# Split output weights kept in DRAM, with the first gathers and two token tiles of the output projection placed beside the end of attention

## The chip, the cores and the metric

The kernel runs on one core of one Trainium2 chip. The metric is device time in microseconds (us), the median of several executions. Five engines work side by side, each through its own queue in order: PE (TensorE) multiplies, ACT (ScalarE), DVE (VectorE) and POOL (GpSimd) do the elementwise work, and SP (SyncE) issues most transfers. POOL issues transfers too, which run through a queue of their own. SBUF is the core's working memory, PSUM holds what PE produces.

## The reference, cut to what matters

One inference step of a decoder with two head groups, a gated short convolution and a sparse attention, for 1024 prompt tokens and 8 sample tokens with 2048 past rows each:

```python
proj = rms_norm(x, norm_g) @ w_in                 # 1024 -> 3864 columns
b_gate, c_gate, conv_in, z_conv, q, kv, gates, z_attn = split(proj)
conv_branch = b_gate * short_conv(c_gate * conv_in) * silu(z_conv)
kv_cmp = compress_blocks(kv rows, cmp_pe, cmp_w)  # 32 rows -> 1, weights cmp_w
o = g0 * attend(q, kv_cmp) + g1 * attend(q, selected) + g2 * attend(q, window)
attn_branch = o * silu(z_attn)
y = x + concat([conv_branch, attn_branch], -1) @ w_out     # 1024 -> 1024
# the sample tokens: the same, with past rows gathered by page_table
# from cache_cmp (compressed with cmp_w) and cache_slc
```

This change touches the way to the last product, `@ w_out`, and to the compression of the gathered past rows with `cmp_w`. Both are computed in two parts each: an operand is split into a high part, rounded to the type float32r, and a low part, the rest. A product is then high*high + high*low + low*high.

## The kernel before

Everything is one program whose order is written by generators; `merge` takes the next piece of the stream that has used the least of its budget, so that the pieces of two streams alternate on each engine's queue. Up to 230 us the input projection for keys, values and queries runs (`phase0`, with `z_part`). From there two streams alternate. The first is attention, `attn_stream`: 32 units, one for each block of 128 queries and pair of heads, four units per block. A unit computes scores (PE, L796), softmax (DVE L784, ACT L786), scaling of the probabilities by gate and sum (POOL, L841 and L845, tiles P0, P1, P2), transposes (PE, L870), a split of the transposed probabilities into `ph` (ACT) and `pl` (DVE), products with the values (PE, L880), and `mixA` (POOL, L895). `copy` (L75) and `sub` (L79) are the helpers that make every high and low part.

The second stream is first the rest of the input projection for the convolution part (`conv_stream`, to about 648 us, with the weight splits `wh` and `wl`). Behind it stands `prefetch`. It loads the eight row blocks of the left half of `w_out` through SP as float32 (`wor`, 256 KB each, L1330), has ACT and DVE split each into `woh` and `wol`, and does the same with the 16 slices of `cmp_w` (`cw_fetch`, four pieces of 4 x 64 KB, tile `cw2`).

When attention has ended, the first stream becomes `out_stream`: for each half n of the output columns and each tile t of 128 tokens it loads x (`xr`), splits the mixed values (`mh` on ACT, `ml` on POOL, from `mixC` for the first four row blocks and from `mixA` for the others), issues 24 matmuls of 512 columns (L1405 to L1407), adds (DVE) and stores (SP). The second stream becomes `cmp_stream`: gathers of past rows through POOL (`raw`, 1 MB each, two buffers), a copy into another order (`reg`, half on ACT, half on POOL), transposes (L999), splits `xh` (ACT) and `xl` (DVE), products with `cw2` (L1023); then `sample_stream` for the 8 sample tokens. In `out_stream` the splits of the right half's weights stand after tiles t = 2 to 5, from loads issued in tiles t = 0 to 3.

`cmp_w` had also been loaded and split once at the beginning (`cw`, in `phase0`), for the prompt's own compression; that copy is given up before attention.

## Time and profile before

| | |
|---|---|
| time, median of 3 runs | 937.73 us (934.72, 937.73, 938.48) |
| the profiled execution | 939.33 us, of which the span of the trace is 937.6 us |
| mean granted PE clock | 0.976 of full speed |
| PE busy | 873.8 us, 93% of the span |
| DVE busy | 619.4 us, 66% |
| ACT busy | 556.0 us, 59% |
| POOL busy | 404.3 us, 43% |
| transfers | 82.24 MB, 47.60 through SP's queue, 33.56 through POOL's |

The profiled execution stands 1.6 us above the median of the three runs, and 1.7 us of it lie outside the span. PE is the busy engine, so what is to be read is where it isn't busy and what it waited for there. In the profile's slices of 23.4 us PE stands at nine tenths or more nearly everywhere from 260 to 650 us; slices 29 and 30 (about 656 to 703 us) show seven and nine tenths.

### The profile page before, as it was taken

The numbers are of one execution on the slowest core, as the hardware profiler recorded it, in microseconds if no ns is written. First come the engines' busy times: TensorE is split into PE (matmuls) and PEld (weight loads), VectorE is DVE, ScalarE is ACT, GpSimd is POOL, SyncE is SP. The second block draws the span as 40 slices with busy tenths as digits, with TensorE's granted clock in tenths as the row PEclk, the third lists the DMA queues.
The fourth block names the chain that finished last, engine by engine and source line by source line (L and its number), as shares of the span: only waits on it lengthen the run. The fifth ranks groups of instructions, "written<-read, shape, count | busy, mean of one in ns | idle before, by whom it ended". The sixth has DMA issues, their size and how long they took to land.

```text
span 937.6 us, 16976 instructions
## 1 busy us (share of the span) xinstructions
PE 873.8 (93%) x5789; PEld 783.2 (84%) x5789; DVE 619.4 (66%) x1714; ACT 556.0 (59%) x1495; POOL 404.3 (43%) x550
## 2 busy tenths in 40 slices
PE   7988999999899999999989999999679999798998
PEld 6888999999689889898979899998568888576765
DVE  5896734788655555856775686577745555877883
ACT  5764543733665655656556666576757666675761
POOL 4132340311454444444434444343455543477761
PEclk8999989999999999999999999999989999899999
DMA  7513331211011000000000100001495661857631
GB/s 246 154 57 95 95 114 35 80 57 31 6 30 34 24 23 24 23 24 23 13 12 23 24 23 1 23 2 44 127 302 182 214 214 47 314 179 226 214 102 47
DMA packets 57955, 82.24 MB, mean 88 GB/s; under 512 B 14470, under 2 KB 43086, under 8 KB 55692
## 3 DMA queue, kind: packets, MB, share of 16 engines
q1 hardware_dynamic: 50956, 47.60, 16.9%
q0 software_dynamic: 6912, 33.56, 10.6%
q8 instruction: 46, 0.75, 0.3%
q14 instruction: 41, 0.34, 0.1%
HBM read 74.24 MB, written 11.10 MB: 91 GB/s over the span
## 4 chain that ended last, share of the span: by engine, by line
PE 49%; ACT 7%; DVE 7%; POOL 3%; issue 3%; DMA 1%; ACTq 0%; DVEq 0%; POOLq 0%
PE o L880 7%; PE pt L870 5%; PE s L796 5%; PE mm L225 5%; PE mm L224 5%; PE mm L223 5%; POOL P L845 2%; ACT P L786 2%; PE mm L1407 1%; PE pt L999 1%; PE mm L1405 1%; PE mm L1406 1%; PE mm L1023 1%; ACT ph L75 1%; PE o L1278 1%
## 5 line engine op out<-in xcount | busy, mean ns | idle before, releaser
L223 PE MATMUL mm<-hH,wh 128*128 128x384 f32 (+1 forms) x480 | 157.9, 329 | 0.0
L225 PE MATMUL mm<-hH,wl 128*128 128x384 f32 (+1 forms) x480 | 155.7, 324 | 0.0
L224 PE MATMUL mm<-hL,wh 128*128 128x384 f32 (+1 forms) x480 | 155.1, 323 | 0.0
L786 ACT ACTIVATE P<-P,stat 128x640 f32<-128x640 f32 (+7 forms) x192 | 112.9, 590 | 37.4 <-DVE stat L784 36.8
L79 POOL TENSOR_TENSOR wl<-wraw,wh 128x256 fp32r<-128x256 f32 (+1 forms) x120 | 87.7, 749 | 106.2 <-ACT wh L75 96.8
L79 DVE TENSOR_TENSOR pl<-pt,ph 128x512 fp32r<-128x512 f32 (+1 forms) x164 | 102.4, 636 | 45.3 <-ACT ph L75 43.9
L75 ACT ACTIVATE ph<-pt 128x512 fp32r<-128x512 f32 (+1 forms) x164 | 88.3, 549 | 66.1 <-PE pt L870 65.5
L845 POOL TENSOR_SCALAR P<-P,stat,gates 128x640 f32<-128x640 f32 (+7 forms) x128 | 101.1, 800 | 55.8 <-DVE stat L836 52.7
L870 PE MATMUL pt<-ident,P 128*128 128x128 f32 x592 | 95.5, 278 | 6.4 <-POOL P L845 3.5
L796 PE MATMUL s<-k,q 128*128 128x320 f32 (+8 forms) x416 | 95.8, 334 | 3.7 <-DVE q L79 1.5
L208 PE MATMUL mm<-wh,hH 128*128 128x256 f32 (+1 forms) x320 | 93.5, 292 | 0.4 <-ACT hH L75 0.4
L209 PE MATMUL mm<-wl,hH 128*128 128x256 f32 (+1 forms) x320 | 93.2, 292 | 0.2
L210 PE MATMUL mm<-wh,hL 128*128 128x256 f32 (+1 forms) x320 | 93.0, 291 | 0.0
L223 PEld LDWEIGHTS mm<-hH,wh 128*128 128x128 f32 x480 | 91.9, 191 | 0.8 <-DVE mixC L693 0.6
L224 PEld LDWEIGHTS mm<-hL,wh 128*128 128x128 f32 x480 | 91.9, 191 | 0.1
L225 PEld LDWEIGHTS mm<-hH,wl 128*128 128x128 f32 x480 | 91.9, 192 | 0.1
L784 DVE CUSTOM_DVE_ANT_0 P<-s,mask 128x32 f32<-128x32 f32 (+8 forms) x160 | 70.9, 473 | 27.0 <-PE s L796 22.4
L870 PEld LDWEIGHTS pt<-ident,P 128*128 128x128 f32 x592 | 70.0, 140 | 19.9 <-POOL P L845 10.1
L880 PE MATMUL o<-ph,v 128*128 128x256 f32 x264 | 74.5, 301 | 3.6 <-ACT ph L75 3.0
L880 PE MATMUL o<-pl,v 128*128 128x256 f32 x264 | 73.3, 300 | 3.3 <-DVE pl L79 3.2
L796 PEld LDWEIGHTS s<-k,q 128*128 128x128 f32 x416 | 66.8, 190 | 8.1 <-DVE q L79 1.7
L841 POOL TENSOR_SCALAR P<-P,stat,gates 128x32 f32<-128x32 f32 x64 | 22.9, 370 | 94.4 <-DVE stat L836 76.4
(342 smaller groups left out, 2182.9 us busy)
## 6 DMA issues: line engine op xcount, KB each, us to landing
wraw<-in_w_in_dram SPq DMA_DIRECT2D x56, 256.0 KB
xt<-in_x_prompt_dram SPq DMA_DIRECT2D x8, 512.0 KB
wor<-in_w_out_dram SPq DMA_DIRECT2D x16, 256.0 KB
xr<-in_x_prompt_dram SPq DMA_DIRECT2D x16, 256.0 KB
out_y_prompt_dram<-xr SPq DMA_DIRECT2D x16, 256.0 KB
sd<-in_state_win_kv_dram SPq DMA_DIRECT2D x8, 512.0 KB
out_s_win_dram<-in_state_win_kv_dram SPq DMA_DIRECT2D x8, 511.0 KB
cwr<-in_cmp_w_dram SPq DMA_DIRECT2D x32, 64.0 KB
```

What stands on the lines that cost most here:

```text
L75: return ACT.activation(out, in_, AF.Copy)
L79: return eng.tensor_tensor(out, a, b, OP.subtract)
L208: PE.matmul(o[:, :n], hH[t // 3][:, k, s], wh, start=k == 0, stop=False)
L209: PE.matmul(o[:, :n], hH[t // 3][:, k, s], wl, start=False, stop=False)
L223: PE.matmul(o[:, :n], wh, hH[c][:, k], start=k == 0, stop=False)
L224: PE.matmul(o[:, :n], wh, hL[c][:, k], start=False, stop=False)
L225: PE.matmul(o[:, :n], wl, hH[c][:, k], start=False, stop=k == 7)
L786: return lambda: ACT.activation(P, P, AF.Exp, bias=stt[:, 0, c:c + 1], scale=-1.0, accum_out=stt[:, 1, c:c + 1])
L796: PE.matmul(s[:, a:b], q[:, i], k, start=first, stop=not first)
L845: POOL.tensor_scalar(P[:, i, :n], P[:, i, :n], stt[:, 2, c + i:c + i + 1], gates[:, qi, gt:gt + 1], op0=OP.mult, op1=OP.mult)
L870: PE.transpose(p[:, y * 256 + i * 128:y * 256 + i * 128 + 128], src[:, i], ident)
L880: PE.matmul(o[0][:, :256], v, X[:, y * 256:y * 256 + 256], start=br == 1 and x == 0 and y == 0 and X is h[0], stop=last and y + 1 == len(p ...
```

## The change

The split forms are made once, written to DRAM (`wo_d`, eight blocks of 512 KB, and `cw_d`, four of 512 KB), and later loaded whole.

- `phase0`: after each of the four splits of `cw` one SP store of the split slices to `cw_d`.
- `attn_stream`: in units 0 to 15 (blocks 0 to 3, whose probabilities need only half of P1) the free half of P1 serves as scratch. An even unit loads a row block of `w_out`; the next odd unit splits it, high part on ACT, low part on POOL, and SP stores it to `wo_d`. P1 becomes two tiles, P1a and P1b.
- `prefetch`: no loads, splits and waits on ACT and DVE any more; POOL issues eight transfers `wo_d` to SBUF and four `cw_d` to SBUF, and the first two gathers between the latter.
- `early_out`: tiles t = 0 and 1 of the left half are put into the second stream, beside attention's last units. Their buffers are the six tiles q0 to q5 that held the queries: tile 0 takes q0 to q4, tile 1 takes q5 and again q0 to q3.
- `first` waits for `early` before it goes on, `out_stream` skips what was begun, and the right half's weight loads move from tiles 0 to 3 to tiles 2 to 5, each behind its tile's store.

```diff
+    wo_d = [dram.tile([128, 2, 512], F32, name=f"wo_d{k}") for k in range(8)]
+    cw_d = [dram.tile([128, 4, 2, 128], F32, name=f"cw_d{i}") for i in range(4)]
...
             if 0 < t < 5:
                 cw_split()
+            if 1 < t < 6:
+                SP.dma_start(cw_d[t - 2], f(cw[:, t * 4 - 8:t * 4 - 4]))
...
+        def w_split(ui):
+            nonlocal wsp
+            if ui % 2 == 0:
+                wsp = at.tile([128, 2, 512], F32R, name="P1b")
+                SP.dma_start(f(wsp[:, 1]), w_out[:, ui // 2, 0:512])
+            else:
+                copy(ACT, wsp[:, 0], f(wsp[:, 1]))
+                sub(POOL, wsp[:, 1], f(wsp[:, 1]), f(wsp[:, 0]))
+                SP.dma_start(wo_d[ui // 2], f(wsp))
...
-            P1 = at.tile([128, 2, 1024], F32, name="P1")
+            a = at.tile([128, 1024], F32, name="P1a")
+            P1 = (a[:, 0:512], a[:, 512:1024]) if u[0] < 4 else (a, at.tile([128, 1024], F32, name="P1b"))
...
+            if u[0] < 4:
+                w_split(ui)
...
     def prefetch():
...
-        cwp = cmp_rooms()
-        jobs = []
         for k in range(8):
-            jobs.append(lambda k=k: w_piece(0, k, cwp, 4))
-            if k % 2:
-                jobs.append(lambda i=k // 2: cw_fetch(cwp, cw2, i))
-        late = []
-        for j in jobs:
-            late.append(j())
-            if len(late) > 4:
-                late.pop(0)()
-            yield 1000
-        for split in late:
-            split()
-            yield 800
+            w = wop.tile([128, 2, 512], F32R, name=f"wo{k}")
+            POOL.dma_start(w, wo_d[k])
+            wo[0, k] = w[:, 0], w[:, 1]
+            yield PREF
+        for i in range(4):
+            if i < 2:
+                gather(i)
+            POOL.dma_start(cw2[:, i * 4:i * 4 + 4], cw_d[i])
+            yield PREF
...
+    def early_out():
+        homes = [f"q{t}" for t in range(6)]
+        def room(name, dt):
+            homes.append(homes.pop(0))
+            return qkv.tile([128, 512], dt, name=homes[-1])
+        for t in range(EARLY):
+            yield from out_tile(0, t, room)
...
-                if n == 0 and t < 6:
-                    if t < 4:
-                        late.append(w_piece(1, t + 4, op, 2))
-                    if t > 1:
-                        late.pop(0)()
+                def made(n=n, t=t):
+                    if n == 0 and late:
+                        late.pop(0)()
+                    if n == 0 and t - EARLY < 4:
+                        late.append(w_piece(1, t - EARLY + 4, op, 2))
...
+    EARLY, PREF = 2, 400
...
         yield from prefetch()
-        done["weights"] = True
+        yield from early_out()
+        done["early"] = True
```

`out_tile` is the body of the loop in `out_stream`, moved out unchanged but for where its buffers come from. The numbers behind names below are those of buffers; a line number of the changed kernel is some 8 to 25 larger than the same statement's before.

**POOL, around the last two units.** Before, from the second half of the scaling of unit 30's P1 to the `mixA` behind that of unit 31's P1:

```order
L845 TENSOR_SCALAR P_8549<-P_8549,stat,gates 128x1024 [waits Activation_49]
L895 TENSOR_TENSOR mixA<-ot,mixA 128x128 [waits DVE_49]
L841 TENSOR_SCALAR P_3452<-P_3452,stat,gates 128x32 [waits DVE_49,PE_49]
L841 TENSOR_SCALAR P_3452<-P_3452,stat,gates 128x32 [waits PE_49,Activation_49]
L845 TENSOR_SCALAR P_8550<-P_8550,stat,gates 128x640 [waits PE_49,Pool_49]
L845 TENSOR_SCALAR P_8550<-P_8550,stat,gates 128x640
L845 TENSOR_SCALAR P_8749<-P_8749,stat,gates 128x1024 [waits DVE_49,PE_49]
L845 TENSOR_SCALAR P_8749<-P_8749,stat,gates 128x1024 [waits Activation_49]
L895 TENSOR_TENSOR mixA<-ot,mixA 128x128 [waits DVE_49]
```

Now, from behind that scaling to the seventh transfer of `wo_d`:

```order
L1369 DMA wo_8849<-wo_d_79 128x1024
L1369 DMA wo_8870<-wo_d_80 128x1024
L903 TENSOR_TENSOR mixA<-ot,mixA 128x128 [waits DVE_49]
L1369 DMA wo_8872<-wo_d_81 128x1024
L1369 DMA wo_8874<-wo_d_82 128x1024
L849 TENSOR_SCALAR P_3470<-P_3470,stat,gates 128x32 [waits DVE_49,PE_49]
L849 TENSOR_SCALAR P_3470<-P_3470,stat,gates 128x32 [waits PE_49,Activation_49]
L853 TENSOR_SCALAR P_8623<-P_8623,stat,gates 128x640 [waits PE_49,Pool_49]
L853 TENSOR_SCALAR P_8623<-P_8623,stat,gates 128x640
L1369 DMA wo_8885<-wo_d_83 128x1024
L1369 DMA wo_8887<-wo_d_84 128x1024
L1369 DMA wo_8902<-wo_d_85 128x1024
```

Two, two and four issues of transfers now stand between the scalings: the eighth is the next row, then comes the scaling of unit 31's P1, then the first gather, `mixA` and the scaling of unit 31's P0 and P2, and then four transfers of `cw_d` with the second gather between.

**PE, at the scores of the last unit.** Before (P are the probabilities of unit 30, `s` the scores of unit 31):

```order
L731 MATMUL mm<-ident,uo 10x128 [waits DVE_49]
L880 MATMUL o<-ph,v_81 128x256 [waits DVE_49,Activation_49]
L796 MATMUL s<-k_80,q_8667 128x512 [waits DVE_49,PE_49]
L870 MATMUL pt<-ident,P_8549 128x128 [waits DVE_49]
L870 MATMUL pt<-ident,P_8549 128x128 x3
L796 MATMUL s<-k_80,q_8668 128x512
```

Now, in the same place:

```order
L739 MATMUL mm<-ident,uo 10x128 [waits DVE_49]
L888 MATMUL o<-ph,v_95 128x256 [waits DVE_49,Activation_49]
L804 MATMUL s<-k_94,q_8740 128x512 [waits DVE_49,PE_49]
L1397 MATMUL mm<-wo_8849,q_8989 128x512 [waits DMASW0_49,Activation_49]
L878 MATMUL pt<-ident,P1a 128x128 [waits DVE_49]
```

The first matmul of token tile 0 stands between a score and the transposes and waits for the first transfer of POOL (DMASW0); the other 23 are spread over the rest of the two units.

**ACT, where attention ends** (`ot` is the last output of attention). Before, with the splits of the weights between:

```order
L75 ACTIVATE woh_9029<-wor 128x512 [waits DMAHW1_49]
L75 ACTIVATE ph<-pt 128x512 [waits DVE_49,PE_49] x2
L75 ACTIVATE cw_8774<-cwr 128x8x64 [waits DMAHW4_49,DMAHW5_49,DMAHW3_49,DMAHW2_49]
L75 ACTIVATE woh_9035<-wor 128x512 [waits DMAHW6_49]
L75 ACTIVATE woh_9039<-wor 128x512 [waits DMAHW7_49]
L75 ACTIVATE ph<-pt 128x512 [waits DVE_49,PE_49]
L75 ACTIVATE ot<-o 64x128 [waits PE_49]
L75 ACTIVATE ot<-o 64x128
L75 ACTIVATE mh<-mixC 128x512
L75 ACTIVATE mh<-mixA 128x512
```

Now:

```order
L75 ACTIVATE q_9096<-mixA 128x512 [waits PE_49]
L75 ACTIVATE ph<-pt 128x512 [waits PE_49,Activation_49] x3
L75 ACTIVATE ph<-pt 128x512 [waits DVE_49,PE_49] x4
L75 ACTIVATE ot<-o 64x128 [waits PE_49]
L75 ACTIVATE ot<-o 64x128
L75 ACTIVATE q_9092<-mixC 128x512 [waits DMAHW6_49,DVE_49]
L75 ACTIVATE reg<-raw 128x8x64 [waits DMASW0_49,Pool_49]
L75 ACTIVATE reg<-raw 128x8x64
```

The weight splits are gone; the high part of token tile 1 (q_9092, in the buffer q0) stands behind attention's last copy and waits for DMAHW6, the store of tile 0's output from that same buffer, and the copies of the gathered rows are queued behind it.

## Rows read from the trace of the kernel before

**Rows 1.** Busy time by stretch: PE, PEld, DVE, ACT, POOL, clock, DMA share, GB/s.

```profile
240.00:440.00 200.00, 193.89 (x1270) 177.13 (x1270) 117.57 (x411) 123.93 (x391) 95.98 (x176) 0.99 0.09 23
...
660.00:680.00 20.00, 13.46 (x74) 10.28 (x75) 14.20 (x30) 12.81 (x31) 11.03 (x12) 0.95 0.42 123
680.00:700.00 20.00, 15.10 (x77) 12.40 (x76) 10.03 (x13) 11.75 (x22) 13.63 (x14) 0.93 0.95 312
...
720.00:900.00 180.00, 168.92 (x1037) 134.69 (x1035) 123.00 (x244) 121.84 (x254) 105.82 (x103) 0.97 0.59 200
900.00:938.00 38.00, 30.86 (x154) 22.16 (x152) 21.52 (x45) 11.59 (x28) 11.00 (x9) 0.99 0.13 43
```

**Rows 2.** Timeline of PE at attention's end: start, duration, operation [idle before <-releaser].

```profile
659.21 0.38 PE L880 MATMUL o<-ph,v 128*128 128x256 f32 x1 [0.18 <-ACT ph L75]
...
664.54 0.38 PE L880 MATMUL o<-ph,v 128*128 128x256 f32 x1 [1.30 <-ACT ph L75]
...
673.71 0.39 PE L880 MATMUL o<-pl,v 128*128 128x256 f32 x1 [0.81 <-DVE pl L79]
```

**Rows 3.** Timeline of PE behind attention.

```profile
678.12 0.63 PE L1405 MATMUL mm<-woh,mh 128*128 128x512 f32 x1
678.55 0.63 PE L1406 MATMUL mm<-wol,mh 128*128 128x512 f32 x1
...
685.66 0.66 PE L999 MATMUL pt<-ident,reg 128*128 128x128 f32 x4 [1.25 <-ACT reg L75]
...
696.23 0.38 PE L1023 MATMUL mm<-xh,cw 128*128 128x256 f32 x1 [2.99 <-ACT xh L75]
...
702.05 0.39 PE L1405 MATMUL om<-woh,mh 128*128 128x512 f32 x1
702.29 0.40 PE L1406 MATMUL om<-wol,mh 128*128 128x512 f32 x1
```

**Rows 4.** Timeline of ACT from attention's end on.

```profile
656.92 0.62 ACT L75 ACTIVATE woh<-wor 128x512 fp32r<-128x512 f32 x1
...
689.99 0.63 ACT L75 ACTIVATE cw<-cwr 128x512 fp32r<-128x512 f32 x1 [0.67 <-DMA cwr<-in_cmp_w_dram]
...
694.54 0.63 ACT L75 ACTIVATE woh<-wor 128x512 fp32r<-128x512 f32 x1 [2.36 <-DMA wor<-in_w_out_dram]
```

**Rows 5.** Timeline of POOL from unit 30 to the first gathers.

```profile
644.23 2.38 POOL L845 TENSOR_SCALAR P<-P,stat,gates 128x1024 f32<-128x1024 f32 x2 [6.68 <-DVE stat L836]
...
659.92 2.39 POOL L845 TENSOR_SCALAR P<-P,stat,gates 128x1024 f32<-128x1024 f32 x2 [5.13 <-DVE stat L836]
...
675.66 1.28 POOL L79 TENSOR_TENSOR ml<-mixC,mh 128x512 fp32r<-128x512 f32 x1 [7.58 <-ACT mh L75]
...
678.75 1.16 POOL L981 DMA_INDIRECT raw<-in_cache_cmp_kv_dram,idx_c  x1 [0.17 <-issue]
```

**Rows 6.** The tile sd, gathers of 512 KB by POOL: durations, and issue to landing.

```profile
L1087 POOL DMA_INDIRECT sd<-in_cache_slc_kv_dram,idx_s x32: 937/956/1910, 807.8 to 893.4; - x32
...
DMA to landing us min/median/max: 5.1/5.6/6.9
```

**Rows 7.** Timeline of SP: the issue of the transfers that ACT waits for at 689.99.

```profile
683.14 2.58 SPq L425 DMA_DIRECT2D cwr<-in_cmp_w_dram x4
```

**Rows 8.** Timeline of PE: a score of unit 31, and two fed steps of compression.

```profile
649.65 0.47 PE L796 MATMUL s<-k,q 128*128 128x512 f32 x1
649.96 0.60 PE L870 MATMUL pt<-ident,P 128*128 128x128 f32 x4
...
705.76 0.60 PE L999 MATMUL pt<-ident,reg 128*128 128x128 f32 x4
...
706.67 0.60 PE L999 MATMUL pt<-ident,reg 128*128 128x128 f32 x4
```

**Rows 9.** Timeline of DVE: a low part, and the sum of a token tile.

```profile
657.66 0.68 DVE L79 TENSOR_TENSOR wol<-wor,woh 128x512 fp32r<-128x512 f32 x1
...
683.98 0.69 DVE L1410 TENSOR_TENSOR xr<-mm,xr 128x512 f32<-128x512 f32 x1 [0.27 <-PE mm L1407]
```

More of the change, by code (lines that the diff above doesn't have):

```diff
@@ L527, in hymba_step_kernel @@
     qt = []
+    qkv = None
     xcp2 = ExitStack()
     def phase0():
+        nonlocal qkv
         x_load(0)
@@ L858, in av_items @@
             k0 = 0 if br == 1 else max(0, qi - 4)
-            ks = [(P[:, :, (kt - k0) * 128:(kt - k0) * 128 + 128], V[br][:, kt, g, :]) for kt in range(k0, qi + 1)]
+            ks = [([p[:, (kt - k0) * 128:(kt - k0) * 128 + 128] for p in P], V[br][:, kt, g, :]) for kt in range(k0, qi + 1)]
             if (qi < 7) == (br == 1):
-                ks.insert(0, (P0, vpc[:, g, :]))
+                ks.insert(0, ([P0[:, i] for i in range(2)], vpc[:, g, :]))
             items = []
@@ L970, in cmp_rooms, with gather @@
         return cwp
+    raws = {}
+    def gather(n):
+        T, qd = divmod(n, 4)
+        r = rawp.tile([128, 2048], F32, name="raw", bufs=2)
+        POOL.indirect_dma_start(out=r, out_offset=None, in_=cache_cmp,
+                                in_offset=bass.IndirectOffsetOnAxis(ap=idx_c[:, T, qd:qd + 1], axis=0))
+        raws[n] = r
     def cmp_stream():
@@ L974, in cmp_stream @@
         cw = cw2
-        raws = {}
-        def gather(n):
-            T, qd = divmod(n, 4)
-            r = cp.tile([128, 2048], F32, name="raw", bufs=2)
-            POOL.indirect_dma_start(out=r, out_offset=None, in_=cache_cmp,
-                                    in_offset=bass.IndirectOffsetOnAxis(ap=idx_c[:, T, qd:qd + 1], axis=0))
-            raws[n] = r
         def regroup(n):
@@ L1005, in transposes @@
             return xh, xl
-        for n in range(2):
-            gather(n)
-        yield 12000
         regroup(0)
@@ L1332, in split @@
         def split():
-            h = wop.tile([128, 512], F32R, name=f"woh{slot}")
-            l = wop.tile([128, 512], F32R, name=f"wol{slot}")
-            copy(ACT, h, r)
-            sub(DVE, l, r, f(h))
-            wo[n, k] = h, l
+            w = (wop if slot < 10 else wop2).tile([128, 2, 512], F32R, name=f"wo{slot}")
+            copy(ACT, w[:, 0], r)
+            sub(DVE, w[:, 1], r, f(w[:, 0]))
+            wo[n, k] = w[:, 0], w[:, 1]
         return split
     def prefetch():
-        nonlocal wop
+        nonlocal wop, rawp
@@ new lines, in prefetch, with out_tile @@
+        for i in range(4):
[3 more added lines that the diff above has]
+            yield PREF
+    begun = set()
+    def out_tile(n, t, room, made=None):
+        begun.add((n, t))
+        cols, s = slice(n * 512, (n + 1) * 512), slice(t * 128, t * 128 + 128)
+        xr = room("xr", F32)
+        SP.dma_start(xr, x_prompt[s, cols])
+        m = []
+        for src in (mixC, mixA):
+            mh, ml = (room(x, F32R).rearrange("p (k c) -> p k c", k=4) for x in ("mh", "ml"))
+            copy(ACT, mh, src[:, :, s])
+            sub(POOL, ml, src[:, :, s], f(mh))
+            m.append((mh, ml))
+        yield 0
+        o = bank("mm")
+        for k in range(8):
+            wh, wl = wo[n, k]
+            mh, ml = (x[:, k % 4] for x in m[k // 4])
+            PE.matmul(o, mh, wh, start=k == 0, stop=False)
+            PE.matmul(o, mh, wl, start=False, stop=False)
+            PE.matmul(o, ml, wh, start=False, stop=k == 7)
+            if k == 3:
+                yield 2600
+        DVE.tensor_tensor(xr, o, xr, OP.add)
+        SP.dma_start(y_prompt[s, cols], xr)
+        if made:
+            made()
+        yield 2600
@@ L1360, in out_stream @@
+    def early_out():
[5 more added lines that the diff above has]
+            yield from out_tile(0, t, room)
     def out_stream():
-        op = ctx.enter_context(pool("out"))
+        nonlocal wop2
+        op = wop2 = ctx.enter_context(pool("out"))
         mS = op.tile([128, 8, 40], F32R, name="mS")
@@ L1380, in sample_half @@
             DVE.tensor_tensor(ys, o[32:40], ys, OP.add)
-        while "weights" not in done:
-            yield None
         late = []
         for n in range(2):
-            cols = slice(n * 512, (n + 1) * 512)
             for t in range(8):
@@ L1389, in out_stream @@
                     yield None
[L1390 to L1415 removed]
+                if (n, t) in begun:
+                    continue
+                def made(n=n, t=t):
+                    if n == 0 and late:
                         late.pop(0)()
[L1417 removed]
+                    if n == 0 and t - EARLY < 4:
+                        late.append(w_piece(1, t - EARLY + 4, op, 2))
+                yield from out_tile(n, t, lambda name, dt: op.tile([128, 512], dt, name=name, bufs=2), made)
             sample_half(n, 0)
@@ L1440, in first @@
         yield from attn_stream()
+        while "early" not in done:
+            yield None
         left.close()
```

36 lines of the change are left out of this document (9 added, 27 removed).

## The prediction

> **What bounds the kernel now.** First the busy times by stretch [rows 1]: PE, the busiest engine, is busy 193.89 of 200 us in attention's first half and 168.92 of 180 us from 720 us on. The hole lies where attention ends: 13.46 of 20 us from 660 on and 15.10 of 20 in the next 20, some 11 us short. So the second view is PE's timeline there, with the waits in brackets. Up to 674.10 (673.71 + 0.39), where attention ends, PE waits ten times for ACT's `ph`, DVE's `pl` and once for POOL, from 0.18 to 1.30 us, together 5.1 us; the first, the longest and the last stand in [rows 2]. Behind it come four losses [rows 3]: before token tile 0, whose last matmul is over at 683.98 [rows 9]; at 678, where matmuls stand 0.43 apart instead of 0.24 (the clock at its lower level, 1.2 instead of 2.4 GHz, for about 3 us); 1.25 us for the first copy of gathered rows; and 2.99 us for `xh` at 696.23. The third view, ACT's timeline, says why the last: ACT, in order, had stood 2.36 us in front of a weight split whose load hadn't landed [rows 4]. The reader is to see that PE's waits before 674 are for ACT and DVE, which also split weights in that time, and that those behind it are for transfers issued late. I count the gain up to one point that both programs pass in the same state: 702.05, tiles 0 and 1 done, seven groups of transposes and five of products of the compression issued.
>
> **Attention's end.** Removed from ACT and DVE are 12 splits, ten of them before 674, at 0.62 us on ACT [rows 4] and 0.68 on DVE [rows 9]: 6.2 and 6.8 us. Added on PE are tile 0's 24 matmuls at 0.24 [rows 3], 5.7 us. PE's own work thus rises by 5.7 us and its waits can fall by 5.1 at most, so the end of attention moves by +0.6 at best and +5.7 at worst. I take +0.6, because what PE waited for is what lost its load, and because the matmuls stand between the very products that waited.
>
> The first of them brings a new wait. It stands behind the score of 649.65, where PE goes on at 649.96 [rows 8], and needs the first block of `wo_d`. POOL can issue that when the scaling of 644.23 is done, at 646.61 [rows 5]. No transfer of this form exists in the trace; the nearest are POOL's gathers of the same 512 KB, 5.1 to 6.9 us from issue to landing, median 5.6 [rows 6]. It lands at 652.2 by the median, and PE, with all of attention queued behind it, waits 2.2 us (1.7 to 3.5 between the ends; nothing at all if a plain transfer takes 3.3). I take +2.2. The other seven blocks are needed from 657 on and have time.
>
> The Trainium skill, "DMA: Bandwidth & Descriptors", section "Anatomy of one DMA — SWDGE (gpsimd) path", fits the time of one transfer by this path as 2.0 us plus its bytes at 436 GB/s, an estimate of 3.2 us for 512 KB. By it the wait vanishes and the sum is 2.2 us better; the gathers of this trace, slower at 5.1 us or more, disagree, so the rows have it.
>
> POOL itself: four issues stand directly ahead of unit 31's scaling at 659.92, for which POOL sat idle 5.13 us [rows 5]. An issue costs 0.96 us (median; 1.91 at most) [rows 6], so four cost 3.8 us and are hidden; at 1.26 us or more little is left, at 1.91 they delay the scaling, and PE's transposes behind it, by 2.5 us. One gather (1.0) then stands ahead of the scaling of P0 and P2, which used to wait about 1.1 us for `mixA`'s input anyway. I take +0.7, with 0 and 3.5 as ends. Attention then ends at 674.1 + 0.6 + 2.2 + 0.7 = 677.6.
>
> **Token tile 1.** It now stands alone behind attention, and its first high part waits for a store. Tile 0's last matmul stands two products or so ahead of attention's end, about 676; its sum on DVE queues behind the last `pl` (0.68 and 0.69 [rows 9]), till 677.2; SP stores; the store must land, because the buffer q0 is to be rewritten. No row has a store's landing. From below it is the issue, about 0.6 us (2.58 for four [rows 7]); from above the 4.3 us from the last issue of four loads, 685.72 [rows 7], to the moment that ACT has them, 689.99 [rows 4], at a DMA share of 0.95 [rows 1]. POOL's transfers of `cw_d` and the second gather, 3 MB, will be partly in flight, so I take 3.0: 680.2. What queues behind the waiting instruction on ACT are the four copies of gathered rows; behind it on PE all of tile 1; on POOL `ml` and its copies. High part 0.62: 680.8. Low part on POOL 1.28 [rows 5]: 682.1. Then 22 matmuls at 0.24, 5.3, and, since PE will have stood for 3 us, 1.3 us for a stretch at the lower clock as at 678.12 (7 matmuls, 0.19 more each). Tile 1 ends at 688.7, where tile 0 ended at 684.0 before. On SP tile 1's store waits for its sum until about 689.5, and the loads of x and of the right half are queued behind it; tile 2, which needs that x only at its end, starts some four steps later, so I cost this at nothing; if ACT meets a weight split before its load has landed, it is the 2.36 us of [rows 4] again.
>
> **The compression.** Its rows are there by then: the first gather is issued near 663, the second near 671, against 678.75 before [rows 5], and landings of 6 us are over at 677. ACT's copies (four at 0.62) fit into tile 1's matmuls. From 688.7 the pipeline fills (transposes 0.36, `xh` 0.6, `xl` 0.7, about 1.9) and then runs at 0.91 us a step, as between 705.76 and 706.67 [rows 8]: five steps, 4.6. The common state comes at 695.2 instead of 702.05, a gain of 6.85. That 2.36 us is not in it, since the right half's splits come later too.
>
> **The making of the split forms.** Units 0 to 15 get eight splits: 0.62 on ACT and 1.28 on POOL each, 15.2 us if all lay on the path, nothing if none did; no gain can come of added work. Nearest is the stretch's own row: POOL is busy 95.98 of 200 us and PE short of full by 6.1 [rows 1], with the convolution's matmuls there to fill. I take 1.0. The SP stores in `phase0` wait for splits with loads queued behind them; their issues are 4 x 0.65 = 2.6 us at most, and the loads run ahead of their use, so 0 (ends 0 and 2.6).
>
> **The sum.** 6.85 - 1.0 = 5.85 us. The profiled execution took 939.33, 1.6 us above the median of the runs: 933.5 on its own scale, 931.9 us as a median. Behind 702 the work is the same, and PE's share of 94% there says that it shifts as a whole.
>
> **The rivals.** About 0.5% (4.7 us, so 933.0) is what a measurement of this kernel can tell from no change.
>
> - The stall only moves. Tile 0's matmuls don't fall into the waits but push attention's end by 3 us more, and the store takes 4.3 us: 4.3 us of the gain go, 936.2 us. For it: each of PE's waits becomes shorter when another one before it delays PE, so 2.2 us at 650 may be all the slack there is, and ACT stands in order behind one store. Against: ten waits, in the same 15 us. Chance 0.27.
> - The splits in units 0 to 15 sit on the path: POOL's `sub` stands just ahead of a unit's scaling, PE's transposes wait for that, and the order of PE's queue leaves no filler at that spot. At 0.85 us each the gain is gone, from 1.45 us each the kernel is slower by over 0.5%, and at the full 1.9 it takes 931.9 + 14.2 = 946 us. For it: in order, an issue or a split ahead of a scaling always delays it. Against: POOL is idle half the time. Chance 0.14.
> - POOL's transfers are slow: eight issues at 1.91, each landing after 6.9, so 1.3 more at the first block, 2.8 more at the scaling, and the store held up by them to 4.3: 5.4 us worse, 937.3. Chance 0.08.
> - The change doesn't do what it says, because what is behind 702 doesn't shift: gathers at a DMA share of 0.59, or the last 38 us, where PE is busy 30.86 [rows 1], set the end. Then about 938. Against: no transfer is late there that PE would meet earlier by more than 7 us. Chance 0.06.
> - The forecast: 0.45.
>
> **Chances and range.** In the forecast's own case the time lies between 926 (no wait at 650, nothing on POOL, no lower clock, splits hidden) and 935; nine tenths of that is below 933 (0.41), and with it a quarter of the first rival's, whose size is uncertain by some 3 us (0.07): faster 0.48. The first, third and fourth rival and the rest give same 0.35; the second and the bad end of the third give slower 0.17. The range 925 to 940 leaves out most of the second rival.
>
> **What would show it.** The trace after should have PE wait about 2 us for POOL's queue near 650; attention's last product at 677 or so; no weight split on ACT and DVE from 655 to 677; a PE gap of about 3 us ahead of tile 1, released by ACT's high part, which was released by a transfer; then transposes without a wait for `reg`, and the third tile's start some 7 us earlier relative to the compression's steps. In units 0 to 15 the scalings should come at the same times within 1 us. Wrong it would be if units 0 to 15 lengthen, if PE's gap at tile 1 is over 6 us, or if the shift present at 700 is not there at 900.

## The result

The changed kernel is slower: 946.10 us (median of 20 runs, 939.97 to 949.18) against 938.99 us (20 runs) for the kernel before, a ratio of 1.0074 with a 95% interval of 1.006 to 1.0089. The forecast was 931.9 us, in a range of 925 to 940. The forecast was wrong in its direction and in its range, although the place at which the gain was expected did give it.

The profiled execution has a span of 943.1 us, 5.5 more than before. Its page gives, for the whole span, busy time, share and instructions:

```profile
PE 878.6 (93%) x5789; PEld 787.1 (83%) x5789; DVE 613.1 (65%) x1702; ACT 549.9 (58%) x1489; POOL 418.8 (44%) x570
```

ACT and DVE do 6 us less, POOL 14 more, PE the same number of matmuls. What has changed most is the clock that TensorE is granted: 0.967 of full speed on average, where it was 0.976. If PE's time at the lower of its two levels (1.2 instead of 2.4 GHz) is counted as half lost, 31.1 us of this span are lost and 22.5 of the one before, an estimate that takes PE to have work in all of that time. So the changed kernel loses 8.6 us more to the clock while its span is only 5.5 longer: the waits that it adds cost less by themselves than by the stretches of lower clock that follow them. The 20 executions say the same (mean clock 0.966, against 0.974 in the executions of the kernel before that ran beside the experiments).

The stretches that answer to [rows 1], shifted by the lag (columns as there):

```profile
250.00:450.00 200.00, 192.39 (x1269) 175.60 (x1269) 116.89 (x395) 126.92 (x388) 106.90 (x184) 1.00 0.19 55
670.00:690.00 20.00, 13.30 (x83) 10.59 (x82) 8.48 (x23) 7.92 (x21) 10.03 (x14) 0.95 0.75 252
690.00:710.00 20.00, 18.28 (x86) 14.44 (x87) 6.07 (x9) 9.89 (x20) 13.19 (x15) 0.88 0.61 207
730.00:910.00 180.00, 167.68 (x1023) 132.94 (x1022) 123.89 (x243) 120.10 (x253) 102.87 (x102) 0.96 0.60 200
910.00:943.00 33.00, 27.11 (x137) 19.18 (x135) 21.05 (x43) 10.69 (x27) 10.38 (x8) 1.00 0.10 34
```

The hole at attention's end has become smaller (18.28 of 20 us in its second half instead of 15.10, though 24 of its matmuls now lie ahead of it), so the loss must lie elsewhere. To find it I took the start of the same matmul in both traces, matched in the order in which PE runs them, and subtracted. That is the lag. Up to 630 us the orders agree nearly everywhere; for 720 us, where they don't, I compared the moments at which the same number of matmul columns is still to be run (weighing each matmul by its time instead moves the entries at 720 by up to 1.1 us). "End" is the difference of the spans. In us:

| kernel | at 101 | at 227 | at 440 | at 629 | at 720 | end |
|---|---|---|---|---|---|---|
| changed | +0.3 | +4.3 | +7.5 | +9.4 | +2.9 | +5.5 |
| predicted | 0 | 0 | +1.0 | +1.0 | -5.9 | -5.9 |

Five steps: +4.0 in the input projection, +3.2 in units 0 to 15, +1.9 at 472 us, -6.5 at attention's end, +2.6 behind it. The estimate of the time lost to the clock, taken over the same stretches, grows by 3.4, 1.7, 1.7, 0 and 1.7 us.

**The input projection.** Two waits of PE for DVE (start, duration, operation, wait), first in the trace before, then in the one after:

```profile
116.25 0.69 PE L489 MATMUL tp<-ident,kd 128*128 128x128 f32 x2 [2.03 <-DVE kd L76]
...
171.09 0.44 PE L489 MATMUL tp<-ident,kd 128*128 128x128 f32 x2 [1.68 <-DVE kd L76]
```

```profile
117.87 0.69 PE L493 MATMUL tp<-ident,kd 128*128 128x128 f32 x2 [2.95 <-DVE rs L199]
...
175.06 0.44 PE L493 MATMUL tp<-ident,kd 128*128 128x128 f32 x2 [1.98 <-DVE rs L200]
```

The waits are longer by 0.9 and 0.3 us, and the clock falls behind them for longer. Two stretches before, then the same two after (columns as in [rows 1], the clock is the third from the end):

```profile
110.00:120.00 10.00, 7.97 (x56) 7.82 (x55) 7.14 (x23) 5.04 (x20) 5.91 (x7) 0.74 0.26 71
120.00:130.00 10.00, 10.00 (x65) 10.00 (x65) 0.86 (x1) 3.85 (x11) 6.17 (x9) 0.75 0.37 91
```

```profile
110.00:120.00 10.00, 7.05 (x56) 6.90 (x53) 5.92 (x23) 6.01 (x23) 3.86 (x6) 0.89 0.71 226
120.00:130.00 10.00, 10.00 (x47) 9.56 (x47) 4.28 (x10) 2.39 (x8) 4.77 (x5) 0.50 0.20 58
```

From 170 to 180 it is 0.83 where it had been 1.00. ACT and DVE show why DVE was late at 117; ACT after, then DVE before and after:

```profile
108.83 0.63 ACT L75 ACTIVATE cw<-cwr 128x512 fp32r<-128x512 f32 x1 [4.59 <-DMA cwr<-in_cmp_w_dram]
...
114.70 0.63 ACT L75 ACTIVATE cw<-cwr 128x512 fp32r<-128x512 f32 x1 [1.57 <-DMA cwr<-in_cmp_w_dram]
```

```profile
114.61 0.27 DVE L267 TENSOR_TENSOR qn<-rows,rs 128x128 f32<-128x128 f32 x1
114.92 0.29 DVE L270 TENSOR_TENSOR ra<-qn,mixC 128x128 f32<-128x128 f32 x1
...
115.90 0.29 DVE L76 COPY kd<-rows 128x256 f32<-128x256 f32 x1
```

```profile
114.58 0.27 DVE L271 TENSOR_TENSOR qn<-rows,rs 128x128 f32<-128x128 f32 x1
115.36 0.69 DVE L79 TENSOR_TENSOR cw<-cwr,cw 128x512 fp32r<-128x512 f32 x1 [0.51 <-ACT cw L75]
115.97 0.86 DVE L274 TENSOR_TENSOR ra<-qn,mixC 128x128 f32<-128x128 f32 x1
...
117.52 0.29 DVE L76 COPY kd<-rows 128x256 f32<-128x256 f32 x1
```

In the kernel before no split of `cw` waits for its load in that stretch: the third and the fourth are made at 122 and 130 us. With the stores in the program they stand at 108.83 and 114.70, among the norms of the keys, and wait there for their loads. The first of these waits, though the longest, costs nothing yet: DVE begins `qn` at 114.58, as before. The second does, because the low part of that split stands on DVE between `qn` and the next step, and `kd`, which PE is to transpose, is made 1.6 us later than before. The products `cc` are done from 112 to 126 us, where they had been spread among the keys' tiles to 133.

**Units 0 to 15.** Three of the eight splits of the output weights stop ACT for their load, and PE behind the last of them:

```profile
268.98 0.63 ACT L75 ACTIVATE P1b<-P1b 128x512 fp32r<-128x512 f32 x1 [1.44 <-DMA P1b<-in_w_out_dram]
...
276.69 0.63 ACT L75 ACTIVATE P1b<-P1b 128x512 fp32r<-128x512 f32 x1 [1.90 <-DMA P1b<-in_w_out_dram]
...
311.83 0.63 ACT L75 ACTIVATE P1b<-P1b 128x512 fp32r<-128x512 f32 x1 [2.99 <-DMA P1b<-in_w_out_dram]
```

```profile
314.59 0.39 PE L888 MATMUL o<-ph,v 128*128 128x256 f32 x1 [1.56 <-ACT ph L75]
```

SP's rows show the chain: the next load goes into P1b only when the store from it has landed, 2.65 us after its issue, and lands some 2.7 us later:

```profile
306.48 0.34 SPq L918 DMA_DIRECT2D wo_d<-P1b  x1
309.13 0.34 SPq L914 DMA_DIRECT2D P1b<-in_w_out_dram  x1
```

**At 472 us** nothing of the change runs; PE waits 1.79 us for DVE in both traces, and after it the clock falls in the changed kernel alone (0.62 from 480 to 484, 1.00 in the kernel before). PE before, then after:

```profile
471.33 0.38 PE L880 MATMUL o<-ph,vpc 128*128 128x256 f32 x1 [1.79 <-DVE stat L784]
```

```profile
478.87 0.39 PE L888 MATMUL o<-ph,vpc 128*128 128x256 f32 x1 [1.79 <-DVE stat L792]
```

**Attention's end.** PE, then ACT and SP:

```profile
660.34 0.48 PE L1397 MATMUL mm<-wo,q 128*128 128x512 f32 x1 [0.54 <-DMA wo<-wo_d]
...
683.04 0.39 PE L888 MATMUL o<-pl,v 128*128 128x256 f32 x1 [0.34 <-DVE pl L79]
...
690.83 0.79 PE L1397 MATMUL mm<-wo,q 128*128 128x512 f32 x1 [7.17 <-ACT q L75]
```

```profile
690.15 0.63 ACT L75 ACTIVATE q<-mixC 128x512 fp32r<-128x512 f32 x1 [5.90 <-DMA out_y_prompt_dram<-q]
```

```profile
683.61 0.36 SPq L1403 DMA_DIRECT2D out_y_prompt_dram<-q  x1
```

Attention ends with the lag that it came with: tile 0's 24 matmuls cost nothing there, and the wait for the first weights is 0.54 us. But the store of tile 0's output, issued at 683.61, lands at 690.1, and until then ACT, and with it POOL and PE, stand in front of q0. PE waits 7.17 us, and the clock is at its lower level for the next 4 us.

### The profile page after: what moved, and what is told of

Its sections match the earlier page's. It is cut to its first block, busy times and chain, and to the rows that moved or that the text cites. A ratio compares the mean times of both kernels' runs of the same rounds, so it can differ in the third digit from the quotient of the medians.

```text
span 943.1 us, 16983 instructions
## 1 busy us (share of the span) xinstructions
PE 878.6 (93%) x5789; PEld 787.1 (83%) x5789; DVE 613.1 (65%) x1702; ACT 549.9 (58%) x1489; POOL 418.8 (44%) x570
## 4 chain that ended last, share of the span: by engine, by line
PE 44%; DVE 8%; ACT 7%; POOL 5%; issue 4%; DMA 2%; ACTq 0%; POOLq 0%; DVEq 0%; SPq 0%
PE o L888 7%; PE pt L878 5%; PE s L804 5%; PE mm L229 4%; PE mm L228 4%; PE mm L227 4%; PE mm L1399 1%; PE mm L1397 1%; PE pt L1025 1%; PE mm L1046 1%; PE mm L1398 1%; PE om L1399 1%; ACT ph L75 1%; PE om L1398 1%; PE om L1397 1%
## 5 line engine op out<-in xcount | busy, mean ns | idle before, releaser
L794 ACT ACTIVATE P<-P,stat 128x32 f32<-128x32 f32 (+5 forms) x128 | 63.9, 499 | 3.6 <-DVE stat L792 3.0
L213 PEld LDWEIGHTS mm<-wl,hH 128*128 128x128 f32 x320 | 62.8, 196 | 1.4 <-POOL wl L79 1.3
L212 PEld LDWEIGHTS mm<-wh,hH 128*128 128x128 f32 x320 | 62.8, 196 | 0.7 <-ACT hH L75 0.7
L214 PEld LDWEIGHTS mm<-wh,hL 128*128 128x128 f32 x320 | 62.8, 196 | 0.2 <-DVE hL L79 0.2
L853 POOL TENSOR_SCALAR P<-P,stat,gates 128x640 f32<-128x640 f32 (+4 forms) x64 | 47.9, 758 | 28.3 <-DVE stat L844 27.8
```

What stands on the lines that cost most here:

```text
L212: PE.matmul(o[:, :n], hH[t // 3][:, k, s], wh, start=k == 0, stop=False)
L213: PE.matmul(o[:, :n], hH[t // 3][:, k, s], wl, start=False, stop=False)
L214: PE.matmul(o[:, :n], hL[t // 3][:, k, s], wh, start=False, stop=k == 7)
L794: return lambda: ACT.activation(P, P, AF.Exp, bias=stt[:, 0, c:c + 1], scale=-1.0, accum_out=stt[:, 1, c:c + 1])
L853: POOL.tensor_scalar(P[i][:, :n], P[i][:, :n], stt[:, 2, c + i:c + i + 1], gates[:, qi, gt:gt + 1], op0=OP.mult, op1=OP.mult)
```

## The experiments

Each starts from the changed kernel, from the kernel before or from the experiment that is named, and was timed beside the kernel before. e1, e2, e3, e5 and e9 leave out the making of split forms and load rows of `w_out` of the same size in their place: they time the rest of the program and are no kernels to use. The ratios are to that kernel in the same runs; its median there was 936.6 to 939.1 us, so 0.1% is 0.94 us.

**e1_no_cw_store: what do the stores in `phase0` cost?**

```diff
-            if 1 < t < 6:
-                SP.dma_start(cw_d[t - 2], f(cw[:, t * 4 - 8:t * 4 - 4]))
...
-            POOL.dma_start(cw2[:, i * 4:i * 4 + 4], cw_d[i])
+            POOL.dma_start(cw2[:, i * 4:i * 4 + 4].rearrange("p a j c -> p (a j c)"), w_out[:, i, :])
```

> The changed kernel without the four stores of cw_d in phase0; cw2 is filled from rows of w_out by transfers of the same number and size, so its numbers are meaningless and its time is that of the rest. Theory A (the stores move the splits of cw and the products cc forward among the keys' tiles, which costs 4.4 us by 184 us into the trace): about 4 us faster than the changed kernel, 942 us, and its lag on the kernel before is 0 at 184 us. Rival (the lag comes from the granted clock falling at other moments, or from transfers running beside, not from the stores): no change, 946 us, or a lag that reappears elsewhere before 230 us.

Measured: 942.04 us, ratio 1.0037 (1.0013 to 1.0061), 3.5 us less than the changed kernel by the ratios. Lag at 227 us: -0.5. The order of the instructions of PE, ACT, DVE and POOL up to the first unit is then that of the kernel before. In this one trace 6.3 us are lost between 227 and 440 us, twice what the changed kernel loses there, so its end tells less than its median.

**e2_no_w_split: what do the splits in units 0 to 15 cost?**

```diff
-            if u[0] < 4:
-                w_split(ui)
...
-            POOL.dma_start(w, wo_d[k])
+            POOL.dma_start(w.rearrange("p a c -> p (a c)"), w_out[:, k, :])
```

> The changed kernel without the eight loads, splits and stores of the output weights in units 0 to 15; the eight blocks are loaded from rows of w_out, with the same number and size of transfers, so the numbers are meaningless. Theory A (three of the splits stop ACT for their load, 6.3 us together, and PE loses 3 us of it between 236 and 316 us): about 3 us faster, 943 us, with no growth of the lag between 236 and 440 us. Rival (the splits sit on the path at every one of the eight places, and the 1.8 us at 472 us is their consequence too): 5 us or more faster, 941 us or less. Rival (they cost nothing, it is the clock): 946 us.

Measured: 942.01 us, ratio 1.0040 (1.0018 to 1.0061), 3.2 us less. The lag grows by 1.4 us between 227 and 440 us instead of 3.2, and not at 472. The rest of 1.4 isn't the splits': the stretch of lower clock near 244 us is longer than before here too, as it is in e3 and e8, which have no split either.

**e3_neither: both left out.**

> Both of the above left out: only the new end of the program is left, with meaningless numbers. Theory A (the parts add): 7 to 9 us faster than the changed kernel, 937 to 939 us, that is 0 to 2 us faster than the kernel before, because the new end gives some 6 us by 705 us and gives 2 to 3 of them back behind 770 us. Rival (the parts don't add, since the filler takes up what either leaves): less than 5 us faster, over 941 us. The prediction on record, whose gain of 6.85 us is all here, would have 932 us.

Measured: 935.39 us, ratio 0.9976 (0.9953 to 1.0000). The two parts together are worth 9.2 us, more than the 3.5 and 3.2 that each gave alone; with the other already gone, the stores are worth 6.0 us (e2 to e3) and the splits 5.7 (e1 to e3). Each difference is good to 2 or 3 us, so the sum can't be told from plain adding. Neither part alone makes the kernel slower, since e1 and e2 are still slower than the kernel before. What is left of the change gains 2.2 us, not the 6.85 that the prediction had for it without its 1.0 for the splits: part of what it placed at the end is missing too.

**e4_other_buffer: the wait for the store.**

```diff
         for t in range(EARLY):
             yield from out_tile(0, t, room)
+            if t == 0:
+                homes.remove("q0")
+                homes.insert(5, "q0")
```

> The changed kernel with one difference: token tile 1 skips buffer q0 and takes q5, q1, q2, q3, q4, so that its first high part waits for tile 0's matmuls and not for the store of tile 0's output. Theory B (PE's wait of 7.2 us ahead of tile 1 is the landing of that store, 6.5 us): the wait falls to about 1 us or none, the stretch of lower clock behind it shortens, 5 to 7 us faster, 940 us. Rival (the next late thing stands right behind: the gathered rows, or the transfers of cw_d, landing after 8 us): PE waits ahead of the transposes instead and it is less than 2 us faster, 944 to 946 us.

Measured: 940.67 us, ratio 1.0020 (0.9993 to 1.0047), 5.1 us less. PE's row ahead of tile 1:

```profile
683.99 0.50 PE L1397 MATMUL mm<-wo,q 128*128 128x512 f32 x1
684.33 0.40 PE L1398 MATMUL mm<-wo,q 128*128 128x512 f32 x1
687.05 0.79 PE L1399 MATMUL mm<-wo,q 128*128 128x512 f32 x1 [2.33 <-POOL q L79]
687.64 0.63 PE L1397 MATMUL mm<-wo,q 128*128 128x512 f32 x1
```

The first two matmuls follow attention without a wait, and the 7.17 us have become 2.33 for the low part, which on POOL stands behind `mixA`. The clock still falls there (0.43 us from one matmul to the next).

**e5_neither_other: e3 and e4 together.**

> e3_neither (no stores in phase0, no splits in units 0 to 15, meaningless numbers) with token tile 1 skipping buffer q0 as in e4_other_buffer: the new end of the program without its own wait and without what is paid for it earlier. If the causes add, the 5.4 us of e4_other_buffer come off e3_neither's 0.24% below the kernel before: 0.8% below it, 930 to 932 us. That would be the prediction on record with its two wrong terms set right. Rival (what the end gains by 720 us is mostly lost again around the sample tokens' selection, whatever its size): no more than 0.5% below the kernel before, as e9_no_early and e10_ahead are, 934 us or more.

Measured: 930.28 us, ratio 0.9937 (0.9916 to 0.9959). Within the noise the causes add (3.7 us between e3 and e5, 5.1 for e4). This is the change with its two mispriced costs and its new wait taken away, 5.9 us below the kernel before. That the prediction had 5.85 is no confirmation: by its own terms it would have had up to 11.2 us for this kernel, since 1.0 for the splits, 3.0 for the store's landing and 1.3 for the clock behind it are gone too.

**e9_no_early: no token tile beside attention.**

```diff
-    EARLY, PREF = 2, 400
+    EARLY, PREF = 0, 400
```

on e3_neither.

> e3_neither (no stores in phase0, no splits in units 0 to 15, meaningless numbers) with no token tile beside attention: what is left of the change is that the weights are loaded split and that the first two gathers come early. Theory F: 4 to 5 us are gained on the kernel before between 640 and 720 us and nearly nothing is given back behind 780, 933 to 934 us, no slower than e3_neither's 935.4, although that one gains 8 us by 720. Rival (the early tiles are worth their 6 us to the end): 939 to 941 us.

Measured: 936.61 us, ratio 0.9977 (0.9955 to 0.9999), the same as e3_neither. With the store's wait the early tiles are worth nothing; without it (e5) 3.8 us. As a test of theory F it speaks against it: this trace, with all 16 tiles left, gives back 2.1 us behind 720 all the same, where those with early tiles and the same pace give back 2.4 to 3.9. It is one trace, the slowest of its twelve executions.

**e8_stores_alone and e11_small_stores: the stores in the kernel before.** The first adds the declaration of `cw_d` and these lines to the kernel before, the second writes 64 KB at a time instead of 512:

```diff
+            if 1 < t < 6:
+                SP.dma_start(cw_d[t - 2], f(cw[:, t * 4 - 8:t * 4 - 4]))
...
+                SP.dma_start(cw_d[t - 2][:, 0, 0], f(cw[:, t * 4 - 8, 0]))
```

> The kernel before with the four stores of the split compression weights in phase0 and nothing else; nobody reads what they write. Theory A: the stores alone move the splits and products and cost 4 to 5 us by 184 us: 942 to 943 us. Rival (their cost comes with the later parts of the change, for example through what depends on them): within 1 us of the kernel before.

> The kernel before with four stores in phase0 at the same places as in e8_stores_alone, of 64 KB instead of 512 KB; the program's order is then nearly that of the kernel before, and the products cc stay interleaved with the keys' tiles. Theory A (the cost of e8_stores_alone, some 5 us, comes with the moved splits and products, or with the traffic of 2 MB): within 1 us of the kernel before, 938 to 940 us. Rival (each store costs by its wait in SP's queue, whatever its size): 4 us or more slower, 943 us.

Measured: 942.42 us, ratio 1.0059 (1.0029 to 1.0089), for the first: the stores alone cost 5.5 us, with PE's row just as in the changed kernel:

```profile
118.40 0.65 PE L491 MATMUL tp<-ident,kd 128*128 128x128 f32 x2 [3.00 <-DVE rs L197]
...
175.68 0.44 PE L491 MATMUL tp<-ident,kd 128*128 128x128 f32 x2 [2.01 <-DVE rs L198]
```

The second was a miss: 941.54 us, ratio 1.0054 (1.0025 to 1.0083), no cheaper with an eighth of the bytes. So it isn't the traffic. But its profiled execution, at 938.85 us one of its fastest, has the wait of 2.03 us at 116, splits of `cw` at 121 and 128 us nearly as in the kernel before, and a lag of only +1.4 at 227. The granted clock of all executions tells the two apart. Counted as in the first section, and against the kernel before beside it, e8 loses 6.5 us more to the clock and 1.1 less otherwise; e11 loses 2.0 to the clock and 2.7 otherwise, each good to about 1 us. So e11's loss is not of the kind that e8 and the changed kernel show. It stays open what it is, and whether theory A's place is the whole of what e8 loses.

**e6_late: a kernel from these findings.** No stores in `phase0`; the compression weights are loaded and split once more beside attention's end, through their old buffer and q5; the output weights' split stands at the end of the odd unit; tile 1 skips q0 as in e4.

```diff
-            if u[0] < 4:
+            if u[0] < 4 and ui % 2 == 0:
                 w_split(ui)
...
             qq = nxt
+            if u[0] < 4 and ui % 2:
+                w_split(ui)
...
+            if k in (1, 3):
+                piece(k // 2)
...
-        for i in range(4):
-            if i < 2:
-                gather(i)
-            POOL.dma_start(cw2[:, i * 4:i * 4 + 4], cw_d[i])
+        for i in range(2):
+            gather(i)
+            late.pop(0)()
+            piece(i + 2)
             yield PREF
```

`piece(i)` is `cw_fetch` into `cw2`; its split is put into `late`, and the last two follow tile 0.

> A complete kernel made from the findings: no stores in phase0 (the compression weights are split once more beside attention's end, four pieces on ACT and DVE, their loads through SP into a buffer of its own and q5); the output weights' splits stay in units 0 to 15, but at the end of an odd unit instead of its start, so that the load has landed; tile 1 skips q0. Theory (the three costs are what the first four runs say): lag on the kernel before about 0 at 230 us, at most +2 at 440, -10 at 720, and about -5 at the end: 933 us. Rival (moving the splits to the end of the unit only moves ACT's wait): lag +5 at 440 us, 937 us.

Measured: 935.13 us, ratio 0.9959 (0.9930 to 0.9989), faster than both. Lag -0.2 at 227 and -8.6 at 720, but +2.8 at 440, so the rival had the point there: in the built program, whose order up to 440 us is that of e1, the splits stand where they had stood, whatever the place in the text, and ACT waits as before (7.3 us in three splits).

**e10_ahead: the load into another buffer, earlier.** From the third block on, on e6_late, with the split back at the unit's start:

```diff
+                if 2 < ui < 15:
+                    wsp = None, qkv.tile([128, 512], F32, name="q0")
+                    SP.dma_start(wsp[1], w_out[:, ui // 2 + 1, 0:512])
```

> e6_late, but from the third block on the row block of the output weights is loaded into the query buffer q0, free by then, as soon as the split before has read it, instead of into P1b after the store from P1b has landed. In e6_late ACT still stood 7.3 us in three splits for their loads, and the lag on the kernel before grew by 3.1 us between 227 and 440 us. Theory (that wait is what the splits cost): ACT's waits for these loads vanish, lag grows by at most 1 us there, 2 us faster than e6_late, 933 us. Rival (the splits cost their place on ACT and POOL, whatever they wait for): the lag still grows by 2 us or more and the time is e6_late's, 935 us.

Measured: 933.50 us, ratio 0.9962 (0.9941 to 0.9984), the same as e6_late; a miss. The lag grows by 5.5 us from 227 to 440. ACT's and SP's rows say that the wait moved and didn't go:

```profile
284.02 0.63 ACT L75 ACTIVATE P1b<-q 128x512 fp32r<-128x512 f32 x1 [3.91 <-DMA q<-in_w_out_dram]
```

```profile
280.12 0.38 SPq L173 DMA_DIRECT2D wraw<-in_w_in_dram  x1
280.55 0.55 SPq L923 DMA_DIRECT2D q<-in_w_out_dram  x1
```

The load now waits on SP behind a load of `wraw`, which waits for its own buffer: POOL's last split of the rows in it ends at 280.09.

**e7_late_so and e12_ahead_so: the pace of the output projection.** e6_late and e10_ahead with one number changed:

```diff
-    SC, SO, SM2, SS = 1.0, 1.9, 1.0, 1.0
+    SC, SO, SM2, SS = 1.0, 2.2, 1.0, 1.0
```

> e6_late with one number changed: each piece of the output projection costs its stream 2.2 instead of 1.9 times its budget, so that the 14 tiles left are spread over more of the sample tokens' work. Theory F (all kernels with two early tiles give back 4 to 6 us between 780 and 940 us because two tiles fewer are left to fill PE while the sample tokens' selection and attention make it wait): less is given back, 2 to 3 us faster than e6_late, 930 us. Rival (what is given back depends on the granted clock, or the sample tokens' transfers, not on filling): within 1 us of e6_late, or slower, if the tail without sample work grows.

> e10_ahead with the output projection's pieces at 2.2 instead of 1.9 of their budget. In e7_late_so this gave back 1.7 us between 720 us and the end where e6_late gave back 6, though their medians were within 0.6 us. If the pacing matters: 1 to 3 us faster than e10_ahead, 931 us. If not: within 1 us of it.

Measured: 934.56 us, ratio 0.9950 (0.9926 to 0.9973), and 933.16 us, ratio 0.9962 (0.9946 to 0.9979). Neither can be told from the kernel that it was made of. The expectation of e12 takes e6 to give back 6 us behind 720; by the table below it is 2.6, and 1.5 in e7, so there was little for the pace to win.

All lags, for the readings above and below:

| kernel | at 101 | at 227 | at 440 | at 629 | at 720 | end |
|---|---|---|---|---|---|---|
| e8_stores_alone | +0.7 | +4.9 | +6.0 | +6.1 | +3.5 | +3.3 |
| e11_small_stores | +0.2 | +1.4 | +2.0 | +1.9 | +0.2 | -0.6 |
| e1_no_cw_store | +0.6 | -0.5 | +5.8 | +5.6 | +0.2 | +4.1 |
| e2_no_w_split | -1.0 | +3.5 | +4.9 | +5.0 | -0.9 | +2.0 |
| e3_neither | +0.2 | -2.1 | -1.5 | -1.2 | -7.1 | -3.9 |
| e4_other_buffer | +0.8 | +5.2 | +8.5 | +9.9 | -0.7 | +3.1 |
| e5_neither_other | -1.2 | -2.3 | -1.9 | -1.6 | -13.1 | -10.7 |
| e9_no_early | +0.2 | -0.9 | +1.1 | +2.5 | -0.9 | +1.2 |
| e6_late | +0.8 | -0.2 | +2.8 | +2.7 | -8.6 | -6.0 |
| e7_late_so | -2.2 | -3.2 | -0.7 | +0.7 | -10.2 | -8.7 |
| e10_ahead | -2.2 | -3.2 | +2.3 | +3.8 | -7.0 | -3.2 |
| e12_ahead_so | +0.7 | -0.3 | +5.0 | +4.9 | -7.2 | -5.9 |

Each is one execution. The eight kernels with an unchanged `phase0` stand between -3.2 and -0.2 at 227 us, the four with the full stores between +3.5 and +5.2: a single lag is good to some 2 us, a group to less. Behind attention e1, e2 and e3 run the same matmuls in the same order as the changed kernel; matched one by one they are ahead of it by 2.7, 3.8 and 10.0 us at 720 and by 2.6, 3.4 and 9.7 at 900.

## Why the prediction was wrong

Between the predicted and the measured trace lie 11.4 us: +0.3 at the start, +4.0 in the input projection, +2.2 in units 0 to 15, +1.9 at 472, +0.4 at attention's end and +2.6 behind it. Two of the signs that it had named for being wrong came plainly, longer units 0 to 15 and a gap of PE over 6 us at tile 1; the third, a shift that is lost by 900, came in part.

**The stores in `phase0`: the step that failed.** The prediction costed them at 0, with 2.6 us as the end, four issues on SP. The runs give 3.5 us (changed kernel against e1), 5.5 (e8) and 6.0 (e2 against e3), above those bounds; each is good to 2 or 3 us, and the eight traces without and the four with the full stores don't overlap at 227 us. I had priced the instructions that were added and the loads queued behind them on SP, and not what stands in another order on ACT, DVE and PE because they are there, nor the clock that falls behind PE's longer wait, 3.4 us of the 4.0 by the estimate. That the splits of `cw` and the products had moved was to be seen in the order before any run; what each would then wait for is the question that wasn't put. That the stores cost this is shown; that the new order is the whole of how they do is not, since e11, with nearly the old order, is as slow.

**The splits in units 0 to 15: a term mis-sized.** 1.0 us was taken, 3.2 us was measured (e2; 5.7 from e1 to e3), inside the bounds of 0 and 15.2 but not in the forecast. POOL's half idle time, from which I argued, was not what mattered: ACT waited 6.3 us for the loads. The prediction looked at two engines' work and not at the latency of a chain of store, load and split through one buffer.

**Attention's end: the mechanism right, the size better than predicted.** +3.5 us was the sum of 0.6, 2.2 and 0.7; the lag goes from +9.4 at 629 to +9.3 at the last product. The new wait for the first weights is 0.54 us, not 2.2, because the plain transfers land faster than the gathers from which I priced them, and POOL's issues cost 0.57 us, not 0.96. POOL's first issue, then the rows of `wo_d` (issue durations in ns; landing in us):

```profile
656.21 1.34 POOL L1369 DMA_DIRECT2D wo<-wo_d  x2
```

```profile
L1369 POOL DMA_DIRECT2D wo<-wo_d x8: 548/566/760, 656.2 to 665.9; - x8
...
DMA to landing us min/median/max: 3.7/4.5/7.0
```

The first of them, the one that PE waits for, took 4.1 us at most (656.21 to PE's start at 660.34), where the gathers' median of 5.6 had been taken for it. The fit of the Trainium skill, "DMA: Bandwidth & Descriptors", section "Anatomy of one DMA — SWDGE (gpsimd) path", gives an estimate of 3.2 us for 512 KB. That is nearer for this one transfer, but no transfer here was that fast, and the median of the eight, 4.5, lies between the two.

**Token tile 1: the mechanism right, the size wrong.** The wait for the store was foreseen with its place and all that queues behind it. Its landing was taken as 3.0 us, between 0.6 and 4.3; it took 6.5, so from attention's end to tile 1's end 15.0 us passed instead of 11.1. In e1, e2 and e3, which have the same wait, it took 6.9 to 7.3. e4 shows that it is this wait: without it 5.1 us come back, and 3.7 between e3 and e5. My upper end came from loads at a DMA share of 0.95; the rows had no store. This one ran beside POOL's transfers of `cw_d`, which themselves took 8 us to land (median) instead of 4.5; that they held it up fits the times, but no run has the store without them.

**The gain itself: there, its size by luck.** From 629 to 720 us the lag falls by 6.5 in the changed kernel; 6.85 was predicted. That it comes so near is luck, since the two errors above, 3.6 us too much and 3.9 too little, cancel. (e8 and e11, whose end is unchanged, fall by 2.6 and 1.7 there, so a part of it may be the execution's own.) In e5, which pays for neither store nor split nor wait, the whole is 5.9 us.

**Behind 720: not the same.** "Shifts as a whole" is wrong by 2.6 us in the changed kernel, and by 2.1 to 3.9 in all kernels with the new end and the old pace, while e8 and e11 keep what they have. Theory F, that two tiles fewer are left to fill PE, has e9 against it. The two kernels with another pace give back 1.5 and 1.3 in their traces, yet their medians are no better. Longer stretches of lower clock near 800 us make 1.7 us of it in the changed kernel, but not in e6, which gives back as much. The cause stays open.

**At 472 us.** 1.9 us in the changed kernel and 1.4 or 1.5 in e4, e7, e9 and e10, where the clock fell behind the wait; next to nothing in e3, e5, e8 and e11, with the same wait (1.76 to 1.79 us), nor in e1, e2, e6 and e12, where it was 1.45. No part of the change was shown to cause it.

**The rivals.** The slower side was given 0.17, for the splits on the path, at 1.45 us each; they are on it with 0.4 each (0.7 from e1 to e3), and the kernel is slower by them together with a cost that was no rival at all. That the second rival's full price, 946 us, is the time measured is chance. "The stall only moves" was true of the store, and a part of what the fourth rival says, that what is behind 702 doesn't shift, came as well.

## What to carry to other kernels

Where a program's order is made by a scheduler, a store added early is not priced by its bytes or its issue: look up in the order which instructions changed places, and for each of them whether its load has landed there, and then time the stores alone, since those of 64 KB cost as much with nearly nothing moved. Price a wait of the matmul engine with the lower clock that may follow it: here, by the estimate above, that was the larger part. Reusing a buffer from which a store has just been issued puts that store's landing on the path of whoever writes next; a list of buffers in turn should skip the one with the store. Work put into idle time of an engine costs little only if its inputs are there, and a load, split and store through one buffer has three latencies in a row.

## What the runs showed of the hardware

A store of 512 KB landed 2.65 us after its issue (306.48 to 309.13), and one of 256 KB needed 6.5 us with three transfers of 512 KB and the end of a gather of 1 MB from POOL's queue still under way (683.61 to 690.15). Plain transfers from POOL cost it 0.57 us each to issue and landed in 3.7 to 7.0 us, where gathers of the same size had cost 0.96 and taken 5.1 to 6.9 [rows 6]. The same wait of PE near 472, 1.76 to 1.79 us, was followed by the lower clock in five traces and not in five others.
